# A decoder block on one core: where VectorE's eight subtractions of a state-space decay stand in its queue

## The chip, the cores and the metric

The kernel runs on one core of a Trainium2 chip. The metric is the device time of one execution in microseconds (us). The engines are named as the profile names them: PE is the matrix engine (TensorE), DVE is VectorE, ACT is ScalarE, POOL is GpSimd, and SP is the engine whose queue issues most of the transfers from HBM. Each engine works through its own queue strictly in order: an instruction that waits holds up everything that stands behind it on that engine. The kernel is written in a tile framework that inserts the semaphores and, unless it is told otherwise, also chooses the order in which instructions enter each queue.

## The reference

One decoder layer over 1024 tokens of width 1024. A normalised input goes through one projection, and its columns feed two parallel mixers, an attention over a sliding window of 128 tokens and a Mamba-2 state-space scan (SSD) in chunks of 128. Their outputs are projected together, and a mixture of 64 small experts follows. The change lies in the scan's decay, here cut to what matters:

```python
a_cs = jnp.cumsum(a, axis=-1)                        # per chunk, per head
seg = a_cs[..., :, None] - a_cs[..., None, :]        # 128 x 128 for each chunk and head
decay = jnp.exp(jnp.where(causal, seg, -jnp.inf))
cb = jnp.einsum("bclgn,bcsgn->bcgls", Cc, Bc)
y_diag = jnp.einsum("bcgls,bcgrls,bcsgrp->bclgrp", cb, decay, xdt)
y_off = jnp.einsum("bclgn,bcgrpn,bcgrl->bclgrp", Cc, prev, jnp.exp(a_cs))

pr = jnp.exp(scores - m)                             # attention, beside it
denom = jnp.sum(pr, axis=-1, keepdims=True) + jnp.exp(sink - m)
out = jnp.einsum("bnhrqk,bnkhd->bnqhrd", pr / denom, vcat)
```

## The kernel before

**Stages.** The tokens are worked in two halves of 512 (four chunks of 128). Each half first projects what all heads share and then runs a loop over eight pairs of heads (`mixer`, from L753). The output projection of each half follows (`project_out`), and after both halves comes the mixture of experts, which streams 1 MB pieces of expert weights.

**The loop over pairs.** PE always has a background stream: the input projection of the next pair, three units of 24 matmuls of 128x512 each (`mm_steps`, L177 with the weights' high part, L181 with the low part). A pair is 72 steps of this stream. The list `events` names places in it, and at each place a piece of the pair's other work is put in; `self.pe(...)` pins an instruction in program order. So PE's order is written by hand. Instructions on other engines that aren't pinned are placed by the scheduler where it expects their inputs to be ready.

**What a pair does, by place.** At 10, `attention_pair` transposes the first half of the probabilities `T` (L579); DVE copies the result out of PSUM under the causal mask (`pc`, L581) and ACT copies it without (`pp`, L583). At 18, PE multiplies both with the values (L592 reads `pc`, L595 reads `pp`). At 20 the second half of `T` is transposed and masked in the same way ("the second mask"), and at 28 PE multiplies it. At 30, `ssd_pair` transposes the scan's input (L443); DVE scales it twice (`xdt` L446, `xde` L449). At 34 and 46 PE makes the next pair's scores (L550) into a PSUM pool of two buffers (`ps_s`); ACT copies the older window out (L554 in the first half's first block, L556 elsewhere) and DVE overlays the other one (L557). At 42 PE multiplies `xde` into the chunk states (L456), and DVE scans them (L460). At 62 PE makes the two parts of the scan's output (L467, and L472, which reads the decays `seg`), and DVE adds them up (`y`, L476 to L478).

**The decay.** `ssd_rows` makes it for a pair. For each of its two heads, a row of cumulated sums is spread over 128 partitions by a transfer from DRAM into a tile `seg` of 128x512 (L415; a pool of three buffers); a third tile `erow` holds the same for the output (L421). At place 50 of a pair the first transfer of the next pair is asked for, at place 66 the rest. Then come, per head, four subtractions on DVE (L427, one for each chunk of 128x128), an exponential on ACT (L431) and a product with `cb` on POOL (L432); the exponential of `erow` (L433) is pinned. Only the first of the eight subtractions is pinned, at place 29.

**Weights of the stream.** For each half unit of 12 steps, SP loads `raw` (L153), ACT makes its high part `whi` (L154) and POOL the low part `wlo` (L155). Each has three buffers.

Of the kernel before, what the change touches and what calls it, by code (L numbers as in the profile page):

```python
# [13 lines left out]
OP = mybir.AluOpType  # L14
# [35 lines left out]
class Block:  # L50
# [356 lines left out]
    def ssd_rows(self, hf, i):  # L407

        nc, fp = self.nc, self.fp
        g = i // 4  # L410
        src = self.acs_d[hf].rearrange("(h c) l -> h (c l)", h=HEADS)
        seg = []
        for h in range(2):
            t = fp.tile([128, NCH, 128], F32, name="seg", bufs=3)
            nc.sync.dma_start(t.rearrange("p c l -> p (c l)"), src[2 * i + h][None].to_broadcast([128, HALF]))  # L415
            seg.append(t)
            if h == 0:
                yield
        erow = fp.tile([128, NCH, 128], F32, name="erow", tag="erow", bufs=1)
        for h in range(2):  # L420
            nc.sync.dma_start(erow[64 * h:64 * h + 64].rearrange("p c l -> p (c l)"),  # L421
                              src[2 * i + h][None].to_broadcast([64, HALF]))
        yield

        for h, t in enumerate(seg):
            for c in range(NCH):
                sub = nc.vector.tensor_scalar(t[:, c, :], t[:, c, :], self.acs[:, c, 2 * i + h:2 * i + h + 1],  # L427
                                              0.0, op0=OP.subtract, op1=OP.min)
                if h == c == 0:
                    self.pe(sub)  # L430
            nc.scalar.activation(t, t, AF.Exp)  # L431
            nc.gpsimd.tensor_tensor(t, t, self.cb[:, g], op=OP.mult)  # L432
        self.pe(nc.scalar.activation(erow, erow, AF.Exp))  # L433
        self.decays = seg, erow
        yield
# [182 lines left out]
    def mixer(self, hf):  # L618
        nc, fp = self.nc, self.fp
# [57 lines left out]
        def gated(i, u, gain):  # L677
            if i % 4 == 0:
                self.gsq = fp.tile([128, HALF], F32, name="gsq", tag="gsq", bufs=1)
            self.add_square(self.gsq, u, i % 4 == 0)  # L680

            def split():
                if i % 2 == 0:
                    t = self.slot(slots["ssd"][i // 2])
                    ssd.extend([t[:, 0], t[:, 1]])
                self.split_scaled(ssd[i], u, gain)


            if i == 6:
                self.split_6 = split  # L690
            else:
                split()

        def attended(i, ot):
            self.add_square(asq, ot, i == 0)
            if i % 2 == 0:
                t = self.slot(slots["att"][i // 2])
                att.extend([t[:, 0], t[:, 1]])
            self.split_scaled(att[i], ot, self.col(C_GATT, i))

        def play(stream, length, events):

            at = 0
            for place, what in events:
                while at < place and next(stream, self) is not self:
                    at += 1
                what()
            while at < length and next(stream, self) is not self:
                at += 1
# [6 lines left out]
        dec = {}  # L716
        step = lambda g: (lambda: next(g, None))

        def load(i):
            dec[i] = self.ssd_rows(hf, i)  # L720
            next(dec[i])
# [3 lines left out]
        A = {}  # L725

        def scores(i):
            A[i] = self.attention_pair(hf, i, q[i])
            next(A[i])

        events = [(at(4), values)]
# [13 lines left out]
        G = {}  # L745
        for i in range(PAIRS):
            def heads(i=i):
                G[i] = self.ssd_pair(i, xs[i], zs[i])
                next(G[i])

            def scanned(i=i):
                next(G[i])
                gated(i, self.u, self.col(C_GSSD, i))  # L753

            def summed(i=i):
                next(A[i])
                attended(i, self.o.rearrange("p c l -> p (c l)"))

            events = [(10, step(A[i])), (18, step(A[i])), (20, step(A[i])),
                      (28, summed), (29, lambda i=i: next(dec[i])), (30, heads), (42, lambda i=i: next(G[i])), (62, scanned)]  # L760
            if i + 1 < PAIRS:
                events += [(34, lambda i=i: scores(i + 1)), (46, lambda i=i: next(A[i + 1])),
                           (50, lambda i=i: load(i + 1)), (66, lambda i=i: next(dec[i + 1]))]
                if i == 4:
                    first_row = self.scale_steps(self.gsq0, 512, "row0", rows, 0)
                    events += [(26, step(first_row)), (44, step(first_row))]
                length = 72
            else:
                last = [self.scale_steps(asq, D, "row2", rows, 2)]
                events += [(48, step(last[0])), (60, step(last[0])),  # L770
                           (94, lambda: last.append(self.scale_steps(self.gsq, 512, "row1", rows, 1))),
                           (94, lambda: next(last[1]))]
                events.append((2, self.split_6))
                stream = self.out_part = self.project_out(hf)
                length = 96
            play(stream, length, sorted(events, key=lambda e: e[0]))
            if i + 1 == PAIRS:
                self.last_row = last[1]
            if i == 3:
                self.gsq0 = self.gsq  # L780
# [791 lines left out]
```

## Time and profile before

| what | value |
|---|---|
| median of the runs | 1835.9 us (1831.87 to 1837.05, 3 runs) |
| the profiled execution | 1837.92 us, of which the span from first to last instruction is 1836.1 us |
| PE, busy share of the span | 92% |
| DVE, ACT, POOL | 42%, 27%, 27% |
| PE waiting for the mask `pc` (L592 behind L581) | 38.1 us in 14 waits |
| loops over pairs, by the start of L443 of their first and last pair | 103.87 to 317.74 us and 503.21 to 722.96 us |

The busy share of PE counts an instruction from its start to its modelled end, so 92% doesn't mean 92% of the peak. The row "PEclk" gives the granted clock of PE in tenths of full speed; it has two levels, 2.4 GHz (1.00 in the rows) and 1.2 GHz (0.50).

### The profile page before, as it was taken

The page shows a single profiled execution, that of the slowest core. Times are in us where ns is not written, and L with a number is a line of the kernel's source. Part 1 is how long each engine was busy: PE and PEld are TensorE (multiplying, and loading weights), DVE is VectorE, ACT ScalarE, POOL GpSimd, SP SyncE. Part 2 cuts the span into 40 slices and gives each one's busy share as a digit, 9 for nine tenths or more (in the row PEclk, how much of TensorE's full clock was granted, in tenths as well). Part 3 has the DMA queues.
Part 4 walks back from the last instruction along what each step waited for, and adds up shares of the span by engine and source line. Part 5 has one row for each costly group of instructions (what it writes and reads, how often), then busy time and mean ns, then how long its engine had stood idle before and what let it go on. Part 6 is the DMA issues. An engine that isn't in the chain of part 4 may idle for free.

```text
span 1836.1 us, 22346 instructions
## 1 busy us (share of the span) xinstructions
PE 1691.1 (92%) x8232; PEld 958.0 (52%) x8232; DVE 772.2 (42%) x1636; ACT 495.7 (27%) x1139; POOL 501.8 (27%) x491
## 2 busy tenths in 40 slices
PE   7899898998998989997999999999989999899896
PEld 5667676876776767876433333333333333333332
DVE  8756666466665666443213223232222221212121
ACT  4455555343555654230002002020010100200201
POOL 5356665762456565430001100000000000000000
PEclk9989999999999999995999999999999999999998
DMA  4222223433222233674999999999999999999994
GB/s 134 82 69 79 77 87 110 127 99 112 69 71 80 70 87 110 223 295 182 420 415 421 414 420 418 419 420 420 420 419 420 419 420 419 420 419 420 419 418 170
DMA packets 109714, 491.51 MB, mean 268 GB/s; under 512 B 14592, under 2 KB 23296, under 8 KB 60448
## 3 DMA queue, kind: packets, MB, share of 16 engines
q1 hardware_dynamic: 93424, 469.02, 65.4%
q0 software_dynamic: 7136, 15.86, 2.3%
q10 hardware_dynamic: 9040, 5.15, 1.0%
q8 instruction: 67, 1.10, 0.2%
q14 instruction: 47, 0.39, 0.1%
HBM read 489.79 MB, written 10.75 MB: 273 GB/s over the span
## 4 chain that ended last, share of the span: by engine, by line
PE 52%; DMA 31%; DVE 12%; issue 2%; ACT 1%; SPq 0%; POOL 0%; DVEq 0%; POOLq 0%; ACTq 0%
PE w L1177 12%; PE acc L177 12%; DMA wt<-in_w_gate_dram 10%; DMA wt<-in_w_up_dram 9%; DMA wt<-in_w_down_dram 8%; PE acc L181 7%; PE w L1220 6%; DMA seg<-acs_d 3%; PE c L1237 3%; DVE seg L427 2%; PE s L550 2%; PE m L592 1%; PE m L595 1%; DVE xs L313 1%; PE t L1061 1%
## 5 line engine op out<-in xcount | busy, mean ns | idle before, releaser
L1177 PE MATMUL w<-wt,xe 128*64 128x512 f32 x2048 | 480.3, 597 | 25.5 <-DMA wt<-in_w_gate_dram 23.7
L177 PE MATMUL acc<-slot,whi 128*128 128x512 f32 x1456 | 403.9, 410 | 10.0 <-DVE xb L306 6.0
L1177 PEld LDWEIGHTS w<-wt,xe 128*64 128x64 f32 x2048 | 156.7, 137 | 330.6 <-issue 271.5
L177 PEld LDWEIGHTS acc<-slot,whi 128*128 128x128 f32 x1456 | 272.2, 193 | 80.0 <-issue 16.0
L155 POOL TENSOR_TENSOR wlo<-raw,whi 128x512 fp32r<-128x512 f32 x184 | 247.7, 1348 | 233.8 <-PE acc L181 104.7
L1220 PE MATMUL w<-wt,hTe 128*64 128x512 f32 x1024 | 241.4, 619 | 0.5 <-DVE hTe L1208 0.5
L1185 ACT ACTIVATE sh<-w,info 128x512 f32<-128x512 f32 x32 | 22.0, 687 | 785.5 <-PE w L1177 785.5
L1141 POOL DMA_INDIRECT xg<-hbuf,sidx x32 | 32.4, 1012 | 724.0 <-DVE ye L1227 693.6
L181 PE MATMUL acc<-slot,wlo 128*128 128x512 f32 x728 | 221.7, 416 | 0.0
L154 ACT ACTIVATE whi<-raw 128x512 fp32r<-128x512 f32 x184 | 115.7, 629 | 221.1 <-PE acc L177 142.0
L181 PEld LDWEIGHTS acc<-slot,wlo 128*128 128x128 f32 x728 | 134.9, 195 | 37.6 <-issue 11.4
L1220 PEld LDWEIGHTS w<-wt,hTe 128*64 128x64 f32 x1024 | 77.8, 142 | 135.8 <-issue 129.0
L1227 DVE SCALAR_TENSOR_TENSOR ye<-w,info,xg 128x512 f32<-128x512 f32 x64 | 67.7, 1099 | 177.2 <-PE w L1220 177.2
L1136 DVE TENSOR_SCALAR GT<-rowno,info 128x192 f32<-128x192 f32 x32 | 10.2, 320 | 285.5 <-PE c L1237 285.5
L1194 DVE SCALAR_TENSOR_TENSOR sh<-w,info,sh 128x256 f32<-128x256 f32 x64 | 28.0, 479 | 195.7 <-PE w L1177 195.7
L1237 PE MATMUL c<-ye,GT 128*128 128x512 f32 (+1 forms) x256 | 95.9, 618 | 0.3 <-DVE ye L1227 0.3
L427 DVE TENSOR_SCALAR seg<-seg,acs 128x128 f32<-128x128 f32 x128 | 59.8, 518 | 38.8 <-DMA seg<-acs_d 33.1
L592 PE MATMUL m<-pc,vd 128*64 128x128 f32 x256 | 37.3, 324 | 38.1 <-DVE pc L581 38.1
L1237 PEld LDWEIGHTS c<-ye,GT 128*128 128x128 f32 (+1 forms) x256 | 27.9, 162 | 66.2 <-issue 64.2
L432 POOL TENSOR_TENSOR seg<-seg,cb 128x512 f32<-128x512 f32 x32 | 43.3, 1352 | 46.8 <-ACT seg L431 46.5
L1151 PE MATMUL t<-ident,xg 128*128 128x128 f32 x256 | 45.8, 307 | 8.7 <-DVE xe L1153 5.0
L313 DVE SCALAR_TENSOR_TENSOR xs<-xb,cw,xs 128x512 f32<-128x512 f32 x48 | 50.2, 1045 | 1.1
(310 smaller groups left out, 1829.0 us busy)
## 6 DMA issues: line engine op xcount, KB each, us to landing
wt<-in_w_gate_dram SPq DMA_DIRECT2D x128, 1024.0 KB, 19.9
wt<-in_w_down_dram SPq DMA_DIRECT2D x127, 1024.0 KB, 20.5
wt<-in_w_up_dram SPq DMA_DIRECT2D x126, 1024.0 KB, 20.5
raw<-in_w_in_dram SPq DMA_DIRECT2D x120, 256.0 KB, 2.6
raw<-in_w_out_dram SPq DMA_DIRECT2D x64, 256.0 KB, 2.7
slot<-in_xT_dram SPq DMA_DIRECT2D x32, 256.0 KB, 5.4
seg<-acs_d SPq DMA_DIRECT2D x32, 256.0 KB, 4.1
erow<-acs_d SPq DMA_DIRECT2D x32, 128.0 KB, 3.9
```

The costliest lines, as they stand in the source:

```text
L154: nc.scalar.activation(hi, raw, AF.Copy)
L155: nc.gpsimd.tensor_tensor(lo, raw, hi.bitcast(F32), op=OP.subtract)
L177: self.pe(self.nc.tensor.matmul(ps, h[:, k, :], acts[k][:, part, :], start=first and k == part == 0, stop=False))
L181: self.pe(self.nc.tensor.matmul(ps, l[:, k, :], acts[k][:, 0, :], start=False, stop=last and k == nk - 1))
L313: nc.vector.scalar_tensor_tensor(acc, xb[:, j:j + HALF], w[:, j:j + 1], acc, op0=OP.mult, op1=OP.add)
L427: sub = nc.vector.tensor_scalar(t[:, c, :], t[:, c, :], self.acs[:, c, 2 * i + h:2 * i + h + 1], 0.0, op0=OP.subtract, op1=OP.min)
L592: self.pe(nc.tensor.matmul(o[hp, blk, :], self.vd[:, blk, hp], pc[:, 2 * h + b, :], start=True, stop=head))
L1151: self.pe(nc.tensor.transpose(ps[:, k, :], self.xg[n % 2][:, 128 * (k4 + k):128 * (k4 + k) + 128], self.ident))
L1177: self.pe(self.nc.tensor.matmul(ps[64 * e:64 * e + 64, :], xe[:, 4 * h + k, SLOTS * e:SLOTS * e + SLOTS], w[e][:, k, :], start=h == k == 0 ...
L1220: self.pe(nc.tensor.matmul(ps[half][64 * e:64 * e + 64, :], hT[:, 2 * j + a, 64 * e:64 * e + 64], w[e][:, a, 512 * half:512 * half + 512], ...
L1227: nc.vector.scalar_tensor_tensor(v(y[:, 512 * half:512 * half + 512]), v(ps[half]), info[:, 2:3], o, op0=OP.mult, op1=OP.add)
L1237: self.pe(self.nc.tensor.matmul(acc[t][half], GT[:, at:at + rows], y[:, 512 * half:512 * half + 512], start=pr == 0, stop=pr == 3))
```

## The change

All eight subtractions of `ssd_rows` are now pinned, and the call that emits them stands at place 21 of the pair, directly behind the second mask at place 20, and no longer at 29. The exponentials and products aren't pinned, but follow their inputs. Nothing is added, removed or resized.

```diff
         for h, t in enumerate(seg):
             for c in range(NCH):
-                sub = nc.vector.tensor_scalar(t[:, c, :], t[:, c, :], self.acs[:, c, 2 * i + h:2 * i + h + 1],
-                                              0.0, op0=OP.subtract, op1=OP.min)
-                if h == c == 0:
-                    self.pe(sub)
+                self.pe(nc.vector.tensor_scalar(t[:, c, :], t[:, c, :],
+                                                self.acs[:, c, 2 * i + h:2 * i + h + 1], 0.0,
+                                                op0=OP.subtract, op1=OP.min))
             nc.scalar.activation(t, t, AF.Exp)
             nc.gpsimd.tensor_tensor(t, t, self.cb[:, g], op=OP.mult)
...
-            events = [(10, step(A[i])), (18, step(A[i])), (20, step(A[i])),
-                      (28, summed), (29, lambda i=i: next(dec[i])), (30, heads), (42, lambda i=i: next(G[i])), (62, scanned)]
+            events = [(10, step(A[i])), (18, step(A[i])), (20, step(A[i])), (21, lambda i=i: next(dec[i])),
+                      (28, summed), (30, heads), (42, lambda i=i: next(G[i])), (62, scanned)]
```

The new text is one line shorter, so what stood at L430 and behind has a number lower by one in the changed kernel. The queues of PE and SP hold the same instructions in the same order as before. Those of DVE, ACT and POOL change.

This is DVE's queue in the second pair of the first half, before. `seg_1007` and `seg_1055` are this pair's two heads, `seg_1281` is the first head of the pair after it; `pc_1093` and `pc_1125` are the two masks:

```order
L319 SCALAR_TENSOR_TENSOR xs_986<-th_995,xs_986 128x512
L427 TENSOR_SCALAR seg_1055<-seg_1055,acs_645 128x128 x4
L668 SCALAR_TENSOR_TENSOR zs_1067<-th_1066,zs_1067 128x512
L427 TENSOR_SCALAR seg_1281<-seg_1281,acs_645 128x128 x3
L581 TENSOR_TENSOR pc_1093<-m_1088,incl_87 128x512
L202 SCALAR_TENSOR_TENSOR slot_1048<-y_1041,prm_78,slot_1048 128x512
L581 TENSOR_TENSOR pc_1125<-m_1120,incl_87 128x512
L446 TENSOR_TENSOR xdt_1179<-m_1174,dt_556 128x512
L202 SCALAR_TENSOR_TENSOR slot_882<-m_1111,prm_78,slot_882 128x512
L427 TENSOR_SCALAR seg_1007<-seg_1007,acs_645 128x128
L449 TENSOR_TENSOR xde_1181<-xdt_1179,dte_653 128x512
```

Seven subtractions stood ahead of the first mask, three of them for the next pair, and the pinned one between `xdt` and `xde`. The same place in the changed kernel:

```order
L319 SCALAR_TENSOR_TENSOR xs_986<-th_995,xs_986 128x512
L667 SCALAR_TENSOR_TENSOR zs_1067<-th_1066,zs_1067 128x512
L580 TENSOR_TENSOR pc_1093<-m_1088,incl_87 128x512
L202 SCALAR_TENSOR_TENSOR slot_1048<-y_1041,prm_78,slot_1048 128x512
L580 TENSOR_TENSOR pc_1125<-m_1120,incl_87 128x512
L427 TENSOR_SCALAR seg_1007<-seg_1007,acs_645 128x128 x4
L427 TENSOR_SCALAR seg_1055<-seg_1055,acs_645 128x128 x4
L445 TENSOR_TENSOR xdt_1179<-m_1174,dt_556 128x512
L448 TENSOR_TENSOR xde_1181<-xdt_1179,dte_653 128x512
L202 SCALAR_TENSOR_TENSOR slot_895<-m_1111,prm_78,slot_895 128x512
```

All eight now stand between the second mask and `xdt`, and the split of the attention's output (L202) has moved behind `xde`.

ACT's queue in the same pair, from the unmasked copy of the second half on, before:

```order
L583 ACTIVATE pp_1127<-m_1120 128x512
L658 ACTIVATE q_1133<-acc_1071 128x512
L489 ACTIVATE sq_1154<-m_1111 128x512
L201 ACTIVATE slot_882<-m_1111,prm_78 128x512
L154 ACTIVATE whi_1206<-raw_1205 128x512
L431 ACTIVATE seg_1007<-seg_1007 128x512
L554 ACTIVATE T_1189<-s_1191 128x128
```

The second head's exponential and that of `erow` stood ahead of the first `pp` there. In the changed kernel:

```order
L582 ACTIVATE pp_1127<-m_1120 128x512
L657 ACTIVATE q_1146<-acc_1071 128x512
L430 ACTIVATE seg_1007<-seg_1007 128x512
L430 ACTIVATE seg_1055<-seg_1055 128x512
L432 ACTIVATE erow_1057<-erow_1057 128x512
L488 ACTIVATE sq_1167<-m_1111 128x512
L201 ACTIVATE slot_895<-m_1111,prm_78 128x512
L154 ACTIVATE whi_1206<-raw_1205 128x512
L553 ACTIVATE T_1189<-s_1191 128x128
```

All three exponentials now stand in a row, ahead of the work on the attention's output, of a weight conversion and of the copy of the next pair's scores. POOL's two products with `cb` have likewise moved together, behind one `wlo` and ahead of the sum of squares (L490) and of the next `wlo`.

## Rows read from the trace of the kernel before

**Rows 1.** The page's first two parts: busy time of an engine with its share and instructions; then the span in 40 equal slices, with the granted clock of PE in tenths and what the transfers moved.

```profile
PE 1691.1 (92%) x8232; PEld 958.0 (52%) x8232; DVE 772.2 (42%) x1636; ACT 495.7 (27%) x1139; POOL 501.8 (27%) x491
...
PEclk9989999999999999995999999999999999999998
...
GB/s 134 82 69 79 77 87 110 127 99 112 69 71 80 70 87 110 223 295 182 420 415 421 414 420 418 419 420 420 420 419 420 419 420 419 420 419 420 419 418 170
```

**Rows 2.** Waits of PE between 80 and 730 us, longest in total first: who waited, for whom, us in total, times, longest.

```profile
PE m L592 <- DVE pc L581: 38.1, 14, 3.4
PE m L579 <- POOL T L571: 3.5, 1, 3.5
```

**Rows 3.** The chain that ended last, in order of time, through the first mask of the fourth pair of the first half: start, us, what.

```profile
179.26 0.69 DVE y L476
...
180.51 3.85 DMA seg<-acs_d
...
184.46 1.92 DVE seg L427 x4
...
186.99 1.60 DVE seg L427 x3
188.58 0.61 DVE pc L581
...
189.24 0.65 PE m L592 x6
```

**Rows 4.** PE's busy time (us, with matmuls in brackets), granted clock, share and rate of the transfers in each of the seven stretches of the first half from one pair's L443 to the next one's, with their sum.

```profile
166.16:195.07 28.91, 26.39 (x161) 1.00 0.29 80
...
226.33:256.13 29.80, 27.28 (x169) 1.00 0.24 73
...
sum 213.87, PE 194.96; mean PE 27.85
```

**Rows 5.** The same for the second half. The stretch shown contains, as the one from 226.33 does, two extra steps that the fifth pair makes (a row of scales).

```profile
629.32:659.64 30.32, 27.53 (x174) 1.00 0.25 71
...
sum 219.75, PE 199.81; mean PE 28.54
```

**Rows 6.** The same columns for four stretches around the wait of the last pair of the first half: before it, the wait, behind it, and behind that.

```profile
300.00:307.16 7.16, 7.16 (x32) 1.00 0.97 282
307.16:310.54 3.38, 0.00 (x0) 1.00 0.77 259
310.70:314.10 3.40, 3.40 (x19) 0.50 0.08 28
314.20:317.70 3.50, 3.50 (x27) 1.00 0.03 6
```

**Rows 7.** The same columns for the first pair of each half, from its first transposes (L579) to L443.

```profile
93.36:103.87 10.51, 10.51 (x56) 0.73 0.22 53
495.11:503.21 8.10, 8.10 (x62) 1.00 0.27 70
```

**Rows 8.** The fourth pair of the first half in order of time: start, us, engine, line, operation, and in brackets the idle time before it with what ended it.

```profile
184.25 0.60 PE L579 MATMUL m<-ident,T 128*128 128x128 f32 x4
...
185.16 1.56 PE L177 MATMUL acc<-slot,whi 128*128 128x512 f32 x6
...
191.66 0.69 DVE L581 TENSOR_TENSOR pc<-m,incl 128x512 f32<-128x512 f32 x1 [1.39 <-PE m L579]
...
192.99 1.27 POOL L155 TENSOR_TENSOR wlo<-raw,whi 128x512 fp32r<-128x512 f32 x1 [0.76 <-issue]
...
195.71 0.69 DVE L446 TENSOR_TENSOR xdt<-m,dt 128x512 f32<-128x512 f32 x1 [3.35 <-PE m L443]
...
197.17 0.69 DVE L449 TENSOR_TENSOR xde<-xdt,dte 128x512 f32<-128x512 f32 x1
197.29 0.63 ACT L431 ACTIVATE seg<-seg 128x512 f32<-128x512 f32 x1 [0.43 <-DVE seg L427]
...
197.82 0.43 ACT L554 ACTIVATE T<-s 128x128 f32<-128x128 f32 x2
...
198.19 0.79 DVE L557 COPY_PREDICATED T<-cur,s 128x256 f32<-128x256 int32 x2 [0.33 <-ACT T L554]
...
199.57 1.05 PE L456 MATMUL m<-xde,Bt 128*128 128x128 f32 x8
...
201.49 1.14 PE L550 MATMUL s<-k,q 64*128 64x256 f32 x8
```

**Rows 9.** The first mask of the second half's first pair in order of time; no subtraction stands near it in DVE's queue.

```profile
495.11 0.60 PE L579 MATMUL m<-ident,T 128*128 128x128 f32 x4
...
495.75 0.69 DVE L581 TENSOR_TENSOR pc<-m,incl 128x512 f32<-128x512 f32 x1 [0.82 <-PE m L579]
...
497.51 0.45 PE L592 MATMUL m<-pc,vd 128*64 128x128 f32 x4
```

**Rows 10.** All subtractions, by their line: shortest, median and longest duration in ns, first and last start, shape.

```profile
L427 DVE TENSOR_SCALAR seg<-seg,acs x128: 273/278/1331, 84.5 to 724.9; 128x128 f32<-128x128 f32 x128
```

**Rows 11.** DVE in order of time in the first half's first pair: four subtractions in a row.

```profile
86.49 0.86 DVE L427 TENSOR_SCALAR seg<-seg,acs 128x128 f32<-128x128 f32 x4
```

**Rows 12.** Waits of DVE between 80 and 730 us, columns as in rows 2.

```profile
DVE xdt L446 <- PE m L443: 48.9, 16, 4.5
...
DVE seg L427 <- DMA seg<-acs_d: 33.1, 14, 5.5
```

## The prediction

> **What bounds the kernel now.** The page's first part comes first: PE is busy for 92% of the span and no other engine for more than 42% [rows 1]. So the question is what PE waits for, and in which stage. From the twentieth of the forty slices to the last but one, transfers run at 415 to 421 GB/s: there the expert weights set the pace. Before that they run at 69 to 134 GB/s for sixteen slices, and PE sets it [rows 1]. The change lies in this earlier part, in the two loops over pairs. The expert stage follows behind both loops and its work is unchanged, so I carry what the loops give back through to the end whole.
>
> The list of PE's waits is next. Between 80 and 730 us one wait stands out: L592, the product of the masked probabilities with the values, waits 14 times for its mask, 38.1 us in all. That is every pair but the first of each half. One more wait, 3.5 us, is for the probabilities themselves (L579 behind POOL's L571) [rows 2]. The chain of waits says why the mask is late. DVE finishes the first part of `y` of the pair before, then a transfer of `seg` takes 3.85 us, then seven subtractions run (1.92 and 1.60 us), and only then the mask, 0.61 us, and PE [rows 3]. The mask itself needs none of this: it reads transposes that PE had finished at 184.85 (184.25 + 0.60), and PE arrived for its result at 186.72 (185.16 + 1.56) [rows 8]. DVE's queue is in order, the subtractions stand ahead of the mask, and they wait for a transfer 33.1 us in all [rows 12].
>
> There is a second price, in the clock. Around the wait of one pair the granted clock is 1.00 ahead of it and during it, 0.50 for 3.4 us of PE's work behind it, and 1.00 again after that [rows 6]. So PE idles and then works at the lower level.
>
> **What the change removes.** Seven subtractions and their transfer no longer stand ahead of the first mask. Only `zs` is left there. What the mask then does is shown by the second half's first pair, where no subtraction is near: the transposes end at 495.71, the mask ends at 496.44 (495.75 + 0.69), and PE starts L592 at 497.51 without a wait [rows 9]. I therefore take the whole 38.1 us as removed, with about 1.1 us of cover per pair.
>
> The first pair of the first half has seven subtractions, and three for the next pair, between the overlay of the scores, the row minimum and the convolution. With them gone the probabilities come earlier than by the 3.5 us that PE waits for them [rows 2]; I take 3.5.
>
> For the clock I use pairs that ran at 1.00 throughout. In the first half such a pair keeps PE busy for 26.39 us, and the one with two extra steps for 27.28, so these steps cost 0.89 [rows 4]. In the second half the pair with the extra steps takes 27.53, so one without takes 26.64 [rows 5]. Seven pairs at these prices are 185.62 us (7 x 26.39 + 0.89) and 187.37 us (7 x 26.64 + 0.89), together 373.0. The sums of PE's busy time are 194.96 and 199.81, together 394.8 [rows 4, 5]. The difference, 21.8 us, is what the lower clock adds. The first half's first pair took 10.51 us at a clock of 0.73 where the second half's took 8.10 at 1.00 [rows 7]: 2.4 us more. Will the clock stay up once the waits are gone? The pairs show stretches at 1.00 of 28.91, 29.80 and 30.32 us even with a wait in them, and the lower level stands right behind a wait where I looked closely [rows 4 to 6]. I take most of it as returned.
>
> Upper end of the gain: 38.1 + 3.5 + 21.8 + 2.4 = 65.8 us. Lower end, with no clock returned: 41.6 us.
>
> **What the change adds.** Eight subtractions stand between the second mask and `xdt`, where one stood behind `xdt`. Who is behind them on DVE: `xdt`, `xde` (PE's L456 waits for it), the split of the attention's output, and the overlay L557. Unhindered, four subtractions take 0.86 us [rows 11], so eight take 1.7. A subtraction takes 278 ns at the median but up to 1331 [rows 10], about a POOL operation of 1.27 us [rows 8]; I count 1.05 us for each such hold. The `wlo` that starts at 192.99, 0.64 us behind the end of the second mask at 192.35, holds one of them; the product of the first head may hold another. So the eight take 2.8 to 3.8 us and end at 195.1 to 196.2. DVE used to wait there for PE's L443, 3.35 us in this pair, until 195.71 [rows 8], and 48.9 us over all sixteen pairs [rows 12]: the subtractions go into time in which DVE had nothing to do. `xdt` then starts at 195.7 to 196.2, and `xde`, now right behind it, ends 1.4 us later at 197.1 to 197.6. It ended at 197.86 before, and PE wants it at 199.57 [rows 8]. Cost: nothing, with 2 us of cover.
>
> The transfer that was waited for now has time: it lands at 184.36 (180.51 + 3.85) [rows 3], and the subtractions that need it can't start before 192.35. SP's queue isn't changed.
>
> On ACT, the last subtraction releases the second head's exponential; behind it stand that of `erow`, the square and split of the attention's output and a `whi`, five instructions of some 0.63 us each [rows 8], 3.2 us, and then the copy of the scores (0.43) and DVE's overlay (0.79). From 195.1 to 196.2 this ends at 199.5 to 200.6, where it ended at 198.98. PE wants the buffer for its second scores at 201.49 [rows 8]. Cover: 0.9 to 1.9 us. This is the thinnest place. The two products on POOL delay one `wlo` by an operation or so; its weights are made ahead, in three buffers, so I cost that at nothing; without that cover it would be 1.3 us a pair.
>
> The last pairs of each half also have the output projection's copies behind the subtractions; I allow a little for that. For a late copy now and then I allow 0.2 us in each of 16 pairs, 3 us, and for a slow stretch or two that remains, 2 us. The bounds of this allowance are 0 and the rivals below.
>
> **Sum.** 65.8 - 5 = 60.8 us. The profiled execution took 1837.9 us with a span of 1836.1; the median is 2.0 below the former. 1837.9 - 60.8 = 1777.1, and 1775 on the scale of the median.
>
> **Rivals.** *The waits go, the lower clock stays.* For it: only the second half's first pair shows such work without a wait [rows 7, 9]. Against it: the lower level stood behind the wait that I looked at, not ahead of it [rows 6]. Price: 41.6 us of gain, 1837.9 - 41.6 - 2.0 = 1794.
>
> *The wait moves to PE's second scores.* ACT's queue has three exponentials ahead of the copy that frees the buffer. If a third hold, or a slower ACT, puts the last subtraction beyond 197.1, PE waits at L550. At 1.5 us in 16 pairs that is 24 us: 65.8 - 24 = 42, some 1794 again; at 0.5 us it is 8 us, and 1778.
>
> *Slower: the subtractions and POOL take turns.* If POOL always had an operation ready and each of the eight were held like the longest, they would take 8 x 1.33 = 10.6 us [rows 10]: `xdt` would start at 203.0, `xde` end at 204.4, and PE's L456 wait 4.8 us instead of the 2.5 us (28.91 - 26.39) that its pair now loses [rows 4]. That is 2.3 us more in 14 pairs and 4.8 in the other two, less 3.5, or 38 us: 1874, with the clock no better. It decides against the change from 8.4 us for the eight on (199.57 + 2.5, less 1.4, less 192.35), 1.05 us each. Against it: after one hold the other three of rows 3's four ran on (1.92 us in all), and POOL's products can't start before the fourth and the eighth subtraction. Here a rule of the Trainium skill speaks against the change: SBUF — State Buffer, section "SBUF: two separate sides", says that VectorE and GpSimd share one pair of ports as an exclusive lock, which whoever starts first keeps for its whole instruction while the other is blocked. By that rule each turn that POOL gets costs a whole operation, as this rival has it; the 1331 ns beside POOL's 1.27 us agree with it.
>
> That the order isn't what the text says is no rival: the queues are listed above.
>
> **How the numbers follow.** Chances: forecast (a gain of 50 to 68 us) 0.72; clock stays 0.10; moved wait that eats more than 15 us 0.10; some new wait that eats all, within 0.3% 0.03; slower 0.05. A difference of 0.3%, 5.5 us, is about what a measurement of this kernel can tell from no change. Faster: 0.72 + 0.10 + 0.10 = 0.92; same 0.03; slower 0.05. The range reaches from the full 65.8 us with some 3 us beyond it, 1766, to the clock and moved-wait rivals, 1797; outside it lie the two last cases and part of the moved wait, somewhat over 0.1.
>
> **What would show it.** In the new profile PE's wait of L592 should be nearly gone from its list, DVE's wait for `seg`'s transfer too, and DVE's wait for L443 should shrink from 48.9 us to under 20. From one L443 to the next it should be 26.4 to 27.6 us at a clock of 0.98 or more. If the clock in these stretches stays at 0.95, the first rival holds; if L550 appears behind L557 or L554 in PE's list, the second; if L456 appears behind `xde` and subtractions average over 1 us, the third. The prediction is wrong in its carrying if the loops shorten by 60 us and the span doesn't.

## The result, and the profile after

| | before | after |
|---|---|---|
| median of the runs (us) | 1835.3 (1831.87 to 1837.05, 4 runs) | 1767.46 (1764.56 to 1771.7, 4 runs) |
| profiled execution, its span (us) | 1837.92, 1836.1 | 1767.88, 1766.2 |
| ratio after to before, 95% interval | | 0.9634 [0.9618, 0.9651] |

The change makes the kernel faster by 67.8 us between medians, and by 69.9 us between the two profiled spans. 1775 us was forecast, within 1766 to 1797. Three executions of the experiments below were far slower than the rest of their kernel (two of about 2075 us, and one of 4756 us of the kernel before) and are left out of every median and ratio.

The page's first parts, columns as in [rows 1]:

```profile
PE 1662.8 (94%) x8232; PEld 934.3 (53%) x8232; DVE 781.0 (44%) x1636; ACT 493.9 (28%) x1139; POOL 516.1 (29%) x491
...
GB/s 130 85 83 98 77 94 136 127 105 109 76 80 102 81 129 203 322 188 370 416 419 415 419 419 419 420 419 419 419 419 420 419 420 420 419 419 420 419 419 158
```

PE has the same 8232 instructions but is busy for 28 us less (1691.1 before): the matmuls themselves became shorter. Most of that is the higher clock. Some of it isn't: behind a late mask the products take longer at the same clock too, as the run with two masks shows below. The expert stage at 415 to 420 GB/s is as it was, only earlier.

PE's waits between 80 and 700 us in the changed kernel, columns as in [rows 2], and the one of DVE's waits there that answers to the first of [rows 12]:

```profile
PE s L800 <- DVE slot L846: 3.3, 6, 2.0
PE m L455 <- DVE xde L448: 2.3, 3, 1.1
PE m L398 <- DVE bc L319: 1.6, 1, 1.6
PE acc L177 <- ACT xb L308: 0.7, 1, 0.7
PE m L594 <- ACT pp L582: 0.3, 1, 0.3
```

```profile
DVE xdt L445 <- PE m L442: 8.9, 12, 0.8
```

The wait for the mask (38.1 us) and the one for `T` (3.5 us) of [rows 2] are gone. DVE's wait for the scan's transposes fell from 48.9 to 8.9 us: the subtractions lie in it. Its wait for the transfer of `seg`, 33.1 us, is not in the list any more. One small wait of PE is new, that for `xde`.

PE in the stretches of the first half from one pair's L442 (L443 before) to the next one's, columns as in [rows 4]:

```profile
151.51:177.48 25.97, 25.97 (x161) 1.00 0.32 91
177.48:204.32 26.84, 26.84 (x169) 1.00 0.30 98
204.32:232.50 28.18, 27.06 (x169) 1.00 0.26 76
...
sum 185.58, PE 184.21; mean PE 26.32
```

The sum was 213.87 us [rows 4]. An ordinary pair takes 25.97 us, all of it busy, at a clock of 1.00, and all fourteen stretches of both halves stand at 1.00. The stretch from 204.32 contains the wait for `xde`.

The fourth pair of the first half in order of time, columns as in [rows 8]:

```profile
174.07 0.69 DVE L580 TENSOR_TENSOR pc<-m,incl 128x512 f32<-128x512 f32 x1 [1.80 <-PE m L578]
...
174.68 2.77 DVE L427 TENSOR_SCALAR seg<-seg,acs 128x128 f32<-128x128 f32 x8
...
175.10 1.28 POOL L155 TENSOR_TENSOR wlo<-raw,whi 128x512 fp32r<-128x512 f32 x1
...
177.41 2.54 POOL L431 TENSOR_TENSOR seg<-seg,cb 128x512 f32<-128x512 f32 x2 [1.02 <-ACT seg L430]
...
178.12 0.69 DVE L445 TENSOR_TENSOR xdt<-m,dt 128x512 f32<-128x512 f32 x1 [0.67 <-PE m L442]
...
178.84 1.65 DVE L448 TENSOR_TENSOR xde<-xdt,dte 128x512 f32<-128x512 f32 x1
...
181.98 1.05 PE L455 MATMUL m<-xde,Bt 128*128 128x128 f32 x8
...
183.90 1.13 PE L549 MATMUL s<-k,q 64*128 64x256 f32 x8
```

Eight subtractions take 2.77 us, one of them held beside POOL's `wlo`, and DVE still waits 0.67 us for PE behind them. `xde` took 0.69 us before [rows 8] and takes 1.65 beside POOL's products: it ends at 180.49, 1.5 us before PE wants it. PE reaches L549 without a wait for the scores' buffer.

In the fifth pair that cover is gone. Same view:

```profile
203.30 1.28 ACT L522 ACT_TABLE_LOAD   x1
...
204.88 1.28 ACT L430 ACT_TABLE_LOAD   x1
...
208.42 0.75 DVE L202 SCALAR_TENSOR_TENSOR slot<-m,prm,slot 128x512 fp32r<-128x512 f32 x1 [2.76 <-ACT slot L201]
...
209.09 0.88 DVE L448 TENSOR_TENSOR xde<-xdt,dte 128x512 f32<-128x512 f32 x1
...
210.11 1.13 PE L455 MATMUL m<-xde,Bt 128*128 128x128 f32 x8 [1.12 <-DVE xde L448]
```

This pair makes the row of scales, with two table loads on ACT around it, between the two exponentials of the decay. That pushes ACT's L201 back, DVE's L202 waits for it, and in this pair L202 stands ahead of `xde`.

**Where the 69.9 us lie**, by the starts of L443 and L442: up to the first pair's, 103.87 before and 99.58 after, 4.3; from there to the first half's last, 213.87 less 185.58, 28.3; between the halves, 185.47 (317.74 to 503.21) less 181.83 (285.16 to 466.99), 3.64; in the second half, 219.75 less 186.86, 32.9; behind the last, 0.8.

The first of these, 4.3, mixes two things. PE comes to the first pair's transposes and to its L443 or L442 at these times, before and after:

```profile
93.36 1.11 PE L579 MATMUL m<-ident,T 128*128 128x128 f32 x4 [3.50 <-POOL T L571]
...
91.70 0.60 PE L578 MATMUL m<-ident,T 128*128 128x128 f32 x4
```

Before, it arrives at 89.86 (93.36 less the wait of 3.50) and reaches L443 14.0 us later; after, it arrives at 91.70 and reaches L442 7.9 us later. So between these two profiles the pair itself gives 6.1 us, and 1.8 us are lost ahead of it. That arrival lies between 89.3 and 91.9 us in thirteen profiles of this study, and nothing ties the 1.8 us to the change. In the run below whose first pair is as before PE arrives at 91.81 and takes 12.1 us, 4.2 more than after the change: it waits 2.8 us there, and the clock behind is 0.84 instead of 0.73.

### The profile page after: what moved, and what is told of

Its sections match the earlier page's. It is cut to its first block, busy times and chain, and to the rows that moved or that the text cites. A ratio compares the mean times of both kernels' runs of the same rounds, so it can differ in the third digit from the quotient of the medians.

```text
span 1766.2 us, 22366 instructions
## 1 busy us (share of the span) xinstructions
PE 1662.8 (94%) x8232; PEld 934.3 (53%) x8232; DVE 781.0 (44%) x1636; ACT 493.9 (28%) x1139; POOL 516.1 (29%) x491
## 4 chain that ended last, share of the span: by engine, by line
PE 36%; DMA 26%; DVE 4%; issue 1%; ACT 0%; POOLq 0%; DVEq 0%; POOL 0%; SPq 0%; ACTq 0%
PE w L1176 13%; DMA wt<-in_w_up_dram 10%; DMA wt<-in_w_down_dram 8%; DMA wt<-in_w_gate_dram 8%; PE w L1219 7%; PE acc L177 4%; PE c L1236 3%; PE acc L181 2%; PE t L1060 1%; PE t L1150 1%; DVE sh L1193 1%; PE t L1122 1%; DVE xe L1152 1%; PE warm L296 1%; DVE slot L846 0%
## 5 line engine op out<-in xcount | busy, mean ns | idle before, releaser
L177 PE MATMUL acc<-slot,whi 128*128 128x512 f32 x1456 | 397.9, 406 | 7.7 <-DVE xb L306 6.0
L155 POOL TENSOR_TENSOR wlo<-raw,whi 128x512 fp32r<-128x512 f32 x184 | 259.8, 1414 | 223.5 <-PE acc L181 92.8
L177 PEld LDWEIGHTS acc<-slot,whi 128*128 128x128 f32 x1456 | 268.6, 190 | 75.4 <-issue 14.3
L181 PE MATMUL acc<-slot,wlo 128*128 128x512 f32 x728 | 215.5, 406 | 0.0
L181 PEld LDWEIGHTS acc<-slot,wlo 128*128 128x128 f32 x728 | 130.5, 189 | 36.8 <-issue 11.4
L565 ACT ACTIVATE T<-T,amin 128x129 f32<-128x129 f32 x128 | 49.5, 388 | 0.0
L1150 PEld LDWEIGHTS t<-ident,xg 128*128 128x128 f32 x256 | 29.2, 149 | 37.3 <-issue 24.0
L1289 POOL DMA_INDIRECT out_dram<-done,idx x16 | 15.6, 973 | 113.3 <-ACT junk L1302 64.6
```

Of the source, the lines that this page charges most:

```text
L155: nc.gpsimd.tensor_tensor(lo, raw, hi.bitcast(F32), op=OP.subtract)
L177: self.pe(self.nc.tensor.matmul(ps, h[:, k, :], acts[k][:, part, :], start=first and k == part == 0, stop=False))
L181: self.pe(self.nc.tensor.matmul(ps, l[:, k, :], acts[k][:, 0, :], start=False, stop=last and k == nk - 1))
L565: nc.scalar.activation(T[:, h, b, :], T[:, h, b, :], AF.Exp, bias=m[:, h, b:b + 1], scale=-1.0, accum_out=den[:, h, b:b + 1])
L1150: self.pe(nc.tensor.transpose(ps[:, k, :], self.xg[n % 2][:, 128 * (k4 + k):128 * (k4 + k) + 128], self.ident))
```

## The experiments

Ratios are to the kernel before, which ran beside them on the same chip with medians of 1834.8 to 1836.8 us.

**The pins without the new place.** The call goes back to place 29; all eight stay pinned.

```diff
-(21, lambda i=i: next(dec[i])),
+(29, lambda i=i: next(dec[i])),
```

> All eight subtractions pinned, but at the old place 29. Theory A (the place behind the second mask is free because VectorE idles there; any later place is not): the first mask is as early as in the change, but the eight now stand between xdt and xde and push xde by 2.7 us, over its cover of some 1.5 us, so PE waits 1 to 2 us at the state product in each of 16 pairs: 1783 to 1800 us. Rival (the pin alone does it, the place is of no account): 1767 us, no wait at the state product.

Measured: 1764.75 us, ratio 0.9612 [0.958, 0.9645]. That is not slower than the change, so between 21 and 29, both behind the second mask, the place isn't what brings the time, and the theory's wait in each of 16 pairs didn't come. The fourth pair in this kernel:

```profile
176.69 0.69 DVE L445 TENSOR_TENSOR xdt<-m,dt 128x512 f32<-128x512 f32 x1 [3.36 <-PE m L442]
177.96 1.65 DVE L427 TENSOR_SCALAR seg<-seg,acs 128x128 f32<-128x128 f32 x8
179.53 0.69 DVE L448 TENSOR_TENSOR xde<-xdt,dte 128x512 f32<-128x512 f32 x1
...
180.55 1.05 PE L455 MATMUL m<-xde,Bt 128*128 128x128 f32 x8
```

Here DVE waits idle for the transposes (46.1 us in 16 waits), then runs eight subtractions in 1.65 us with no hold, since POOL has nothing at that place. `xde` ends 0.3 us before PE wants it. In the last pair of each half one subtraction is held beside a `wlo`, the eight take 2.68, and PE waits 1.9 us for `xde`.

**The new place without the pins.** The kernel before, with its one pinned subtraction called at place 21 instead of 29.

> Place 21, but only the first of the eight pinned, as before the change. Theory A: the scheduler again puts seven ahead of the first mask and nothing is gained: 1835 us, PE waits for the mask some 38 us. Rival (the earlier place does it): near 1767 us.

Measured: 1841.39 us, ratio 1.0029 [1.0012, 1.0046]. The other seven stand ahead of the first mask as before. PE's and DVE's waits between 80 and 730 us:

```profile
PE m L592 <- DVE pc L581: 39.9, 14, 3.4
```

```profile
DVE seg L427 <- DMA seg<-acs_d: 28.0, 12, 5.7
```

Both are much as before [rows 2, 12]. With the run above: it is the pins that bring the gain, at either place behind the second mask.

**Pinned ahead of the first mask, with three and with five buffers of `seg`.** Does the late transfer make the mask late, or the subtractions ahead of it?

```diff
-(21, lambda i=i: next(dec[i])),
+(9, lambda i=i: next(dec[i])),
...
-name="seg", bufs=3
+name="seg", bufs=5
```

The second edit is in the second of the two kernels only.

> All eight pinned ahead of the first mask (place 9), three seg buffers, so that the second head's transfer still lands late. Theory A (work that waits for the late transfer stands ahead of the mask): VectorE waits for the transfer, then eight subtractions of 2.7 us, then the mask some 1.2 to 2 us after PE arrives, with slow clock behind many waits: 1785 to 1815 us. Theory B (any work ahead of the mask costs the same, landed or not): the same time as with five buffers.

> As the one with three buffers, but five seg buffers, so that both transfers of a pair are asked for a pair earlier. Theory A: no wait for the transfer, the eight fit into the time before the transposes end, the mask is in time: 1767 to 1778 us and VectorE's wait for the seg transfer near 0. Theory B: 1785 us or more, the same as with three buffers.

Measured: 1850.53 us, 1.0076 [1.0052, 1.01], and 1851.11 us, 1.0082 [1.005, 1.0114]. PE's wait for the mask is 45.0 us in 13 waits in both, and in neither does DVE wait for the transfer of `seg`. Theory A's times were too low by 35 us and by 73. Theory B's equal times came, but three buffers have no wait for the transfer here either, so the two runs don't say what a late transfer adds. What they show is that a mask behind subtractions can be late even when their data are there. A pair of the kernel with five buffers in order of time:

```profile
181.69 1.75 POOL L155 TENSOR_TENSOR wlo<-raw,whi 128x512 fp32r<-128x512 f32 x1
182.21 4.74 DVE L427 TENSOR_SCALAR seg<-seg,acs 128x128 f32<-128x128 f32 x8
...
183.41 1.26 POOL L489 TENSOR_TENSOR gsq<-gsq,sq 128x512 f32<-128x512 f32 x1
184.63 1.25 POOL L155 TENSOR_TENSOR wlo<-raw,whi 128x512 fp32r<-128x512 f32 x1
...
186.87 0.68 DVE L580 TENSOR_TENSOR pc<-m,incl 128x512 f32<-128x512 f32 x1
...
187.60 1.12 PE L591 MATMUL m<-pc,vd 128*64 128x128 f32 x6 [3.81 <-DVE pc L580]
```

POOL has three operations in a row here, and three of the eight subtractions take about 1.3 us each, the other five about 0.27. They start only 1.6 us before PE wants the mask (187.60 - 3.81 = 183.79), since they stand behind `zs`. Unheld, in the 1.65 us of place 29, they would still have made the mask some 0.75 us late, by an estimate from these rows; POOL's three holds add 3.1. In the two pairs of the first half that lack the sum of squares (L489), POOL has two, and the eight take 3.7 us. This is the "take turns" rival's mechanism: one subtraction is held for each operation that POOL has queued, and not all eight. The kernel before, with the transfer early and its queue otherwise as it was, was not run. SBUF — State Buffer, section "SBUF: two separate sides" of the Trainium skill, says that the engine that doesn't hold the shared port pair is blocked for the other's whole instruction; the holds of 1.3 us beside POOL's operations of 1.25 to 1.75 us agree.

**The first pair as before.** All subtractions pinned, but in the first pair of each half only the first one.

```diff
+                if i or h == c == 0:
+                    self.pe(sub)
```

> The changed kernel, but in the first pair of each half only the first subtraction is pinned, so that the scheduler may put seven early again. Theory (the first half's first pair gave 4.3 us and the stretch ahead of the second half's first pair 3.7 us): 1775 us, with PE's 3 us wait for the convolution's copy and the 3 us wait for the probabilities back. Rival (the fourteen later pairs gave everything): 1767 to 1769 us.

Measured: 1773.05 us, 0.9652 [0.9632, 0.9673], beside 1767.11 us, 0.9626 [0.9606, 0.9646], for the changed kernel run again in the same place:

> The changed kernel itself, beside the other three on the same chip: 1767 us, both theories.

So the two first pairs are worth 5.9 us, where the theory had 8. By spans up to the last pair it is 4.15 before the first L443 (103.87 against 99.72) and 2.46 between the halves (184.31 against 181.85), of the 3.64 that the kernel before loses there. PE's waits, where two are back:

```profile
PE acc L177 <- ACT xb L308: 3.0, 1, 3.0
PE m L579 <- POOL T L571: 2.8, 1, 2.8
```

The first of them is the second half's, and the same 3.0 us stood in the list of the kernel before. There, in order of time:

```profile
452.38 2.47 DVE L427 TENSOR_SCALAR seg<-seg,acs 128x128 f32<-128x128 f32 x7 [5.55 <-DMA seg<-acs_d]
...
454.77 0.68 DVE L674 COPY v<-m 128x512 f32<-128x512 f32 x1
454.88 0.63 ACT L431 ACTIVATE seg<-seg 128x512 f32<-128x512 f32 x1 [2.51 <-DVE seg L427]
455.41 0.58 ACT L308 ACTIVATE xb<-acc 128x512 f32<-128x512 f32 x1
...
456.05 2.59 PE L177 MATMUL acc<-slot,whi 128*128 128x512 f32 x8 [3.04 <-ACT xb L308]
```

Seven subtractions wait for their transfer, ACT's exponential waits for them, and the copy `xb` that frees PE's buffer stands behind that exponential in ACT's queue. PE is held at 453 us by a decay that it first reads at 515.51 (L472).

**The first mask issued several times.** The changed kernel with 2, 3, 4 and 6 masks where there is one. It makes PE wait for the mask with no subtraction and no transfer in play, and so tests the cover and the clock.

```diff
+            for _ in range(2 if bp == 0 else 1):      # 3, 4, 6 in the others
                 nc.vector.tensor_tensor(pc, pt, self.incl[:, None, :].to_broadcast([128, 4, 128]), op=OP.mult)
```

> The changed kernel, but the first mask of each pair is computed six times over with the same result, some 3.2 us more on VectorE, no transfer involved. Theory (PE's wait, whatever causes it, brings the lower clock behind it): PE waits 2 to 2.5 us in 16 pairs, 32 to 40 us, and the clock in the loops falls to 0.93 to 0.96, another 15 to 25 us: 1814 to 1832 us. Rival (the clock fell for a reason of its own in the kernel before): the same waits at a clock of 0.98 or more, 1799 to 1807 us.

> The changed kernel, with the first mask of the probabilities issued twice in every pair (the output is the same). That measures the cover of the mask in the changed kernel. One more mask is 0.71 us ahead of what PE waits for; the run with six masks waited 4.35 us in most pairs for 5 x 0.71 more masks and for the step of 1.69 us that the queue then put between them (5.24 together), so the mask has some 0.9 us of cover, and a second one should fit in it. Theory (a cover of 0.9 us): no wait of PE for the mask in most pairs, clock 1.00 in them, 1767 us, within 3. Rival (the mask is already on the edge, and each microsecond on VectorE ahead of it shows in the end): 16 x 0.7 = 11 us more, 1778, and more if the clock falls too.

> The changed kernel, with the first mask issued three times. Two more masks (1.42 us) and the step of 1.69 us that then lies between them make 3.1 us; less a cover of 0.9 us PE should wait some 2.2 us in each pair, 16 x 2.2 = 35 us. Theory 1 (any such wait is followed by a stretch at the lower level, at 1.7 us lost in each): 15 x 1.7 = 25 us on top, 1767 + 35 + 25 = 1827, and a clock under 1.00 in nearly all pairs. Theory 2 (a wait of 2.2 us isn't followed by it, those of before of 2.5 us and more were): 1802, and a clock of 1.00 in nearly all pairs.

> The changed kernel, with the first mask issued four times: 2.13 + 1.69 - 0.9 = 2.9 us of wait in each pair, about the waits of the kernel before (2.5 to 3.4 us), 16 x 2.9 = 46 us. If the wait alone is what brings the lower clock, whatever caused it, the clock is under 1.00 in nearly all pairs as it was before, and the time is 1767 + 46 + some 25 = 1838, that of the kernel before. If the lower clock of the kernel before came from something else that the change took away, it stays at 1.00: 1813.

| masks | median (us) | ratio | PE's wait for them in all | in most pairs | stretches from pair to pair under a clock of 1.00 |
|---|---|---|---|---|---|
| 1 (the change, again) | 1767.11 | 0.9626 [0.9606, 0.9646] | none | none | 0 of 14 |
| 2 | 1776.74 | 0.9683 [0.9664, 0.9701] | 2.4 | none | 0 of 14 |
| 3 | 1829.2 | 0.9971 [0.9959, 0.9982] | 37.1 | 2.2 | 12 of 14 |
| 4 | 1844.45 | 1.0052 [1.0036, 1.0068] | 49.4 | 2.9 | 13 of 14 |
| 6 | 1874.49 | 1.021 [1.0185, 1.0235] | 73.6 | 4.4 | 14 of 14 |

Of the theories, "any such wait is followed by a stretch at the lower level" came out with three masks (1827 forecast) and within 7 us with four (1838). With six the waits were about twice what was forecast and the time 42 us above its range; the clock fell as the theory had it, to 0.90 to 0.95 in the stretches. With two, the median is near the rival's 1778, though the clock stayed at 1.00 and the profiled execution took only 1770.8.

Two neighbouring stretches with three masks, columns as in [rows 4], both with a wait of 2.18 us in them:

```profile
129.76:159.87 30.11, 27.93 (x161) 0.94 0.29 80
159.87:188.41 28.54, 26.36 (x161) 1.00 0.26 84
```

The same work costs 1.57 us more where the lower level follows the wait. With the kernel's own waits of 2.5 to 3.4 us replaced by waits of the same size that have another cause, four masks give back the whole gain, though they make 16 waits where there were 14. So it is the wait that brings the lower level, whatever PE waits for, and a wait of 1.1 us (the change's fifth pairs) didn't. The run with the pins at place 29 lies between: its two waits of 1.93 us, for `xde` in the last pairs, were followed by 1.00 in the second half, and in the first by

```profile
287.69:291.10 3.41, 3.41 (x13) 0.54 0.11 43
```

with 1.00 ahead of the wait. Why a wait of one size is followed by the lower level in some places and not in others (2.2 us in 12 stretches of 14) stays unexplained.

With two masks the theory of 0.9 us of cover fell: the pair takes 26.33 us instead of 25.97 in the first half, and 26.83 instead of 26.19 in the second, with no wait for the mask. The pair behind 152.09 us there:

```profile
171.07 1.40 DVE L581 TENSOR_TENSOR pc<-m,incl 128x512 f32<-128x512 f32 x2
...
172.56 0.60 ACT L583 ACTIVATE pp<-m 128x512 f32<-128x512 f32 x1 [0.69 <-DVE pc L581]
172.62 0.62 PE L592 MATMUL m<-pc,vd 128*64 128x128 f32 x6
...
173.21 0.13 PEld L595 LDWEIGHTS m<-pp,v 128*64 128x64 f32 x1 [0.22 <-ACT pp L583]
```

The mask itself is in time, by 0.15 us. But ACT's unmasked copy `pp` starts only when DVE's `pc` is done, and it ends at 173.16; the weight load of PE's first L595 waits 0.22 us for it. From its first product to the next step of the stream PE takes 1.18 us (172.62 to 173.80), where the changed kernel takes 0.86 in the same pair (172.00 to 172.86). In the first pair of each half PE waits 0.7 us for the mask, but there `zs` has come between the two masks, and the second ends 1.8 us behind the first: a cover of 1.1 us.

**Each place where it costs nothing.** Place 29 in all pairs but the last of each half, 21 there.

```diff
-(21, lambda i=i: next(dec[i])),
+(21 if i + 1 == PAIRS else 29, lambda i=i: next(dec[i])),
```

> All eight pinned at place 29, and at place 21 in the last pair of each half alone. Theory (any place behind the second mask serves as long as PE finds xde in time; at 29 POOL holds no subtraction, in the last pair 21 is better): no wait at the state product of more than 0.5 us, 1758 to 1764 us. Rival (the places differ by nothing that can be measured): 1765 to 1768 us.

> Pins of the changed kernel, the step at its old place 29, and at place 21 in the last pair of each half alone: the same kernel as the run with both places, for a profile without a disturbance. Expected 1762 to 1764 us, some 4 us below the changed kernel: no wait of PE for the probabilities' masks, none of 1.9 us for xde in the last pair of each half (place 29 had them), none of 1.1 us for it in the fifth pairs (place 21 has them). If the two places differ only by what a measurement can't tell, it lies within 2 us of the changed kernel.

Measured: 1762.92 us, 0.9598 [0.9576, 0.9621], and again 1760.73 us, 0.9599 [0.9584, 0.9614]. The waits for `xde` shrink to 0.2 us in all, and the fifth pairs take 26.85 and 27.07 us instead of 28.21 and 28.36 in the changed kernel's second run: 2.65 us less. It is the fastest kernel of this study, some 4 to 6 us below the change, which is about as little as can be told apart. Of the 6.5 us between the two profiled spans (1764.1 and 1757.6) 2.6 lie in the loops. Another 2.1 lie ahead of the first pair's transposes (PE arrives at 89.78 us against 91.84) and 1.9 behind the last pair, and nothing ties these to the edit.

## Why the prediction was right, and where its sizes were off

**The waits of 38.1 and 3.5 us, right.** Both left PE's list, and the seven subtractions ahead of the first mask were the cause: with one pin alone the wait for the mask comes back whole (39.9). The working told them as late through their transfer as well. How the 38.1 us split between the transfer and the seven themselves stays open. At place 9 DVE waited for no transfer, with three buffers or with five, and the mask was late all the same, for the most part through POOL's holds. But that is another queue than the one before, where DVE did wait for the transfer, in the fourth pair 1.95 us of the 2.52 that PE waited:

```profile
184.46 1.92 DVE L427 TENSOR_SCALAR seg<-seg,acs 128x128 f32<-128x128 f32 x4 [1.95 <-DMA seg<-acs_d]
```

Both reasons lead to the same 38.1 us, since both go when nothing stands ahead of the mask, so the forecast didn't depend on which it is.

**The clock, 21.8 us, right but for some 2 us.** All fourteen stretches stand at 1.00. Priced with the extra steps in two stretches of each half (below), the same sum gives 20.0 instead of 21.8. The doubt, whether it would stay up without the waits, is settled by the repeated masks: waits alone bring it down. The rival in which it stays low has nothing left for it.

**The sum of 65.8 us was too small an upper end.** The spans differ by 69.9. That 1767 us still lies in the range, 1.5 us inside its lower end, owes something to the 3 us that it was given beyond the sum. First, the fourteen stretches: 38.1 + 21.8 = 59.9 was taken, 28.3 + 32.9 = 61.2 was measured, and the agreement hides two errors that cancel. The price of an ordinary stretch, 26.39 and 26.64 us [rows 4, 5], came from stretches with a wait in them; without it they take 25.97 and 26.19. The pair with two masks, 26.33, shows where that lies: a late `pc` makes `pp` late too, and PE's products of the two then take about 0.3 us longer. That is 7 x 0.42 + 7 x 0.45 = 6.1 us too dear. Against it, the extra steps lie in two stretches of each half and not in one (x169 beside x161 above), 2 x 0.88; the last stretches take 26.64 and 26.69, 1.2 more; and the fifth pairs' waits for `xde` cost 2.65: 5.6 us too cheap. The rest is small waits that the 38.1 left out: the stretches' lengths less PE's busy time are 433.6 - 394.8 = 38.8. Second, the first pairs: 3.5 + 2.4 = 5.9 was put down to the first half's alone. From PE's arrival on that pair gave 6.1; up to its end it is 4.3, because PE came to it 1.8 us later. Another 3.64 came from the second half's, and the working had nothing for it. The working took that pair as free of subtractions [rows 9], which holds for its mask but not for the stretch of 50 us ahead of it. Its wait of 3.0 us, and a stretch of 3.4 us at the lower level from 457.5 on behind it, stood in the trace and weren't followed back. Third, the allowance of 5 us for late copies and slow stretches: of such mishaps only the waits for `xde` came, 2.65.

**The cost of eight subtractions, right.** 2.8 to 3.8 us with one or two holds was forecast; 2.67 to 2.77 with one hold in all but the last pairs, measured. They end in DVE's idle time, as forecast.

**The covers.** The thinnest place was named as PE's second scores; no wait came there. It is `xde`, for which 2 us was counted: 1.5 us in an ordinary pair, since `xde` itself is held by POOL's products (1.65 us instead of 0.69), and less than nothing in the fifth. That ACT loads tables between the two exponentials there, and that L202 stands ahead of `xde` in the fifth pairs alone, the working passed over. The 1.1 us of cover of the mask were 0.9 for `pc`, by the waits (three masks: 2 x 0.71 + 1.69 of L202, less 2.18), but the 0.71 us of a second mask already cost 0.36 a pair, so `pp` has only about 0.35.

**The rivals.** *Take turns* has a true mechanism and a wrong price: not 8 x 1.33 = 10.6 us, but one hold per operation that POOL has in its queue, three at place 9 (4.74 us), one at 21 (2.77), none at 29 (1.65) outside the last pairs. *The moved wait* came at another place, with 2.3 us in all, for `xde`. The carrying held: behind the last pair only 0.8 us differ, and the loops' gain reached the end whole.

## What to carry to other kernels

An instruction that its consumer needs late, and that a scheduler may move, costs where it lands in an in-order queue; pin the whole group, not its first member, and look at each engine that waits on the group (here DVE's mask and ACT's copy `xb`, two places with the same cause). A wait of the matrix engine is priced with what follows it: here waits of 2.2 us and more were mostly followed by 3.4 us at half the clock, another 1.6 us. When a group of VectorE operations is placed, count what GpSimd has queued at that place, since here each of its operations of 1.25 us or more held one of them.

## What was not expected of the hardware

A subtraction of 0.28 us takes about 1.3 us when it meets a long operation of POOL, but then one subtraction slips in at each change from one POOL operation to the next: eight beside three of them take 4.74 us, not eight times 1.3. The loop ran at a clock of 1.00 throughout once no wait of more than 1.1 us was left in it. With four masks, waits of 2.9 us in most pairs were followed by the lower level in 13 of 14 stretches, while the transfers ran at 67 to 82 GB/s outside the last stretch of each half, as in the kernel before (71 to 83).
